# A macaron transformer layer in split fp32: step order of the down products, two loads, a layer norm and the block preparations are moved

## The chip, the cores and the metric

The kernel runs on one core of one Trainium2 chip. The metric is the device time of one execution in microseconds (us). TensorE (PE) multiplies, PEld is its weight load, VectorE is DVE, ScalarE is ACT, GpSimd is POOL, and SP issues nearly all DMAs. PSUM banks hold the sums that PE accumulates.

## The reference

One layer on x of 256 tokens by 2048 channels, in float32, every matrix product of full width:

```python
x = x + 0.5 * swiglu(rmsnorm(x, g1), w_gate, w_up, w_down)      # hidden width 5632
h = rmsnorm(x, gm)
q, k, v, u, vs, g_att, g_sg = split(h @ w_in)                   # 11776 columns
att = merge of 3 dilated causal window attentions (4 heads each) @ w_att_out
vs  = layernorm(gelu(vs)); sg = (gelu(u) * (tril(sg_w) @ vs + sg_b)) @ w_sg_out
x = x + (sigmoid(g_att) * att + sigmoid(g_sg) * sg) @ w_out
x = x + 0.5 * swiglu(rmsnorm(x, g2), w_gate2, w_up2, w_down2)
out = rmsnorm(x, gf)
```

Some 461 MB of weights are read from HBM once.

## The kernel before, in words

**Split products.** PE works on a rounded form of fp32. Each weight tile is therefore split in two: ACT copies it into `wh` (the rounded part, L351) and DVE writes `wl` = tile − `wh` (L66 is the line of a helper through which all DVE instructions go). The left side is kept as such a pair as well: `xhi`/`xlo` for normed x, `hA`/`hB` for the hidden layer, `mhi`/`mlo` for the merged branches. Each product is the sum of three matmuls of 128x512: high with `wh`, high with `wl`, low with `wh` (L358).

**Steps.** The products are cut into steps, and `lay_out` writes one list of all steps ahead of time. A plain step multiplies 256 rows of a 512-column weight strip with both halves of the tokens: 12 matmuls. Two neighbouring strips make a pair with four banks, `qd_0`, `qd_1` (first strip, token halves 0 and 1) and `qd_2`, `qd_3` (second strip). For a part of the rows a pair uses a seven-product scheme for 2x2 blocks in place of eight products: a *quad* with products p1 to p7, of 2 or 3 column groups each (6 or 9 matmuls). It loads four weight blocks (b11, b21, b12, b22, tiles `quads`, `part`, `vs`), and DVE forms sums of them: f, t2, t1 and t4 (tile `sum` holds t2 and then t4). It also needs sums of the left side's blocks (`forms`: `fx`, `fy`, `fh`, made by `sums_of` over a tile `fs`). p1, p6 and p7 stand near the end of the pair before (`opening`), p5, p4, p3 and p2 near the start of the pair itself (`closing`). After p1, p6, p7 and p5 a bank is read and moved or corrected by ACT or DVE before PE may add into it again: after p5, DVE writes `qd_2` = `qd_3` + something.

**Order within a pair.** The last argument of `gemm` that matters here is a pair (size, stage). With a stage function, plain steps are sorted by it: `PAIR` sorts the steps q of m in three stages (all but the last four, the next two, the last two), so that the steps of the first strip and of the second alternate by stage. It serves where the left side is still being made: x in four parts c = 0 to 3, the hidden layer by strips.

**Queues.** PE, ACT, DVE and SP each run their instructions in the order of the program. `split(i)` runs up to 5 steps ahead of PE, as far as a ring of 9 tiles of `wh`/`wl` has room. Five buffers of `raw` weights are refilled as splits free them. `at(e, fn)` puts a piece of work after step time e. `extra(wait, slack, cost, fn)` lets DVE work wait for a moment when its estimated load is low. `prepare_ready` forms the next block sum when the blocks it needs were issued 3 step times ago and DVE's load is low; `prepare_for` forces it when the split is due.

**x turned around.** Normed x is needed with channels on partitions. `turn` transposes 32x32 squares on DVE (`bt`), writes them to DRAM (`bm`, L471), reads them back shifted (L477, four DMAs `xt<-bmx` or `ga<-bmm`), and `ev` scales and splits them (`xt<-xt,gcols`, `xhi`, `xlo`). `turn_x` does so for a quarter c of x when a stage ends (n = 1: into the mixer; n = 2: into the second SwiGLU), `post_merge` for `m`. `sums_of` for n = 1 takes its tile `fs` from tag `gate`, two buffers that `bt` and `xt` use as well.

**The mixer's own loads.** At fixed step times after the mixer starts come the first quad blocks of the mixer (`gates`, +5), the spatial weights (+7) and the layer norm's rows (+10). The layer norm of `vs` is six pairs of DVE instructions (`nrm`).

Of the kernel before, what the change touches and what calls it, by code (L numbers as in the profile page):

```python
# [22 lines left out]
KD = D // P  # L23
FF = 5632
NC = 512
# [19 lines left out]
RAWB = 5  # L45
# [26 lines left out]
def layer(ctx: ExitStack, tc: tile.TileContext, a, out):  # L72
# [75 lines left out]
    def lay_out():  # L148
# [28 lines left out]
        for kind, s in steps:  # L177
            width = 2 if kind == "n" else s[0]["nq"]
            t += 1 if kind == "n" else width / 4
            ends.append(t)  # L180
            slots.append([(pos + q) % RING for q in range(width)])
            pos += width
            if kind == "n":
                hus.append(s)
                s[0]["steps"] += 1
            else:
                s[0]["gemms"][s[1] in ("p3", "p5", "p6", "p7", "p1")]["steps"] += 1
# [15 lines left out]

    PAIR = (2, lambda p, q, m: 2 if q >= m - 2 else q >= m - 4)
    BOTH = (2, None)
# [109 lines left out]
    def prepare_ready():  # L315
        for quad in started:
            if not quad["todo"]:
                continue
            what = quad["todo"][0]
            blocks, forms = NEEDS[what]  # L320
            if (all(quad["loaded"].get(b, 1e9) + 3 <= now[0] for b in blocks) and quad["split"].issuperset(forms)
                    and DVE.load + 0.56 * quad["nq"] * (NC / 512) <= FULL):
                assert all(b in quad["loaded"] for b in blocks)
                prepare_next(quad)
# [5 lines left out]

    started = []

    def form_of(quad, form):
# [211 lines left out]
    def residual(e, n, c, banks, scale, norm):  # L545
# [16 lines left out]

        turn_x(e + (6 if c == 1 else 2), n, c, 7 if c == 3 else 6)

    def turn_x(i, n, c, lag, read=3):
        def evac(src):
# [4 lines left out]
            split_psum(hi, lo, src, 1 if n and c < 3 else 0)  # L571
            tag = "gate" if n == 1 else "tmp"
            if c == CS[n]:
# [13 lines left out]
    def ffn(wg, wu, wd, down_post, group):  # L587
# [10 lines left out]
        for after, (part, quads_of) in zip(GATES, enumerate(PARTS)):  # L598
            for f in range(*after):
# [46 lines left out]
                quad = dict(k0=4 * CS[n], nq=2 if late else 3, forms=xT, home=merge if late else home)  # L646
                gemm(wg, f * NC, 0, KD, lhs_x, post_gate, BOTH if f else PAIR, bank, quad)
                gemm(wu, f * NC, 0, KD, lhs_x, post_up, BOTH, bank, quad)
# [67 lines left out]
    def post_gelu(key, j):  # L716
        def post(e, banks):
# [24 lines left out]
            if key == "vs":  # L742
                at(e + 2, st)
                if j == 2:
                    for t in range(NT):
                        for jj in range(3):
                            def nrm(t=t, jj=jj):
                                s = slice(jj * NC, (jj + 1) * NC)
                                v = mix["vs"][:, t, s]
                                DVE.scalar_tensor_tensor(v, v, mix["mv"][:, t, 0:1], mix["lng"][:, s],  # L750
                                                         op0=OP.subtract, op1=OP.mult)
                                DVE.scalar_tensor_tensor(v, v, mix["lnrs"][:, t:t + 1], mix["lnb"][:, s],
                                                         op0=OP.mult, op1=OP.add)
                            at(e + 4 + 3 * t + jj, nrm)
                    spatial_operands(e + 11)
# [257 lines left out]
    def post_merge(c):  # L1013
        def post(e, banks):
# [15 lines left out]

            turn(e + 2, f"m{c}", 8, put_tokens(lambda: ga), lambda: flat(ga), ev)
        return post

    front = [(o_s + j * NC, post_gelu("vs", j)) for j in range(3)] + [(o_u + j * NC, post_gelu("u", j)) for j in range(3)]
    for j, (c0, post) in enumerate(front):
        if j < 2:
            gemm(w_in, c0, 0, KD, lhs_x, post, PAIR if j == 0 else (1, None))
            continue
# [98 lines left out]
    at(88, masks)  # L1137
    at(mixer + 7, spatial_weights)
    at(mixer + 10, layer_norm_rows)
    for h in range(2):  # L1140
        sgw_turn(mixer + 13 + 8 * h, h)
    at(ends[-1] - 36, load_fin)
    for after, home in ((16, homes[0]), (mixer + 5, gates), (start_of(ffn2_gate) + 1, homes[1])):
        at(after, lambda home=home: move_in(home))
# [55 lines left out]

    loaded, done = RAWB + MORE, 3

# [98 lines left out]
```

## Time and profile before

| what | value |
|---|---|
| median of 3 runs | 2014.53 us (2013.36 to 2017.0) |
| the profiled execution's own time | 2012.44 us |
| its span, first to last instruction | 2010.7 us |
| mean granted TensorE clock | 0.995 |
| busy: PE, PEld, DVE, ACT, POOL | 1981.1, 1732.3, 1594.0, 1188.5, 52.5 us |
| HBM read | 461 MB, 244 GB/s with writes over the span |

The profile names a wait by the engine and tile that ended it. The stages lie thus in the span: first SwiGLU to about 700 us, the mixer's front to 970, attention to 1050, branches and merge to 1255, `w_out` to 1350, second SwiGLU to the end.

### The profile page before, as it was taken

What the parts mean: (1) busy time and instruction counts of PE and PEld (TensorE: products, weight loads), DVE (VectorE), ACT (ScalarE), POOL (GpSimd) and SP (SyncE); (2) the same over time, 40 slices, a digit from 0 to 9 for tenths busy, and PEclk for the clock granted to TensorE, in tenths of its full rate; (3) what the DMA queues carried; (4) which work ended last, traced back from release to release, by engine and by line L of the source; (5) the groups of instructions that cost most, each with busy time, mean ns of one, the idle gap of its engine ahead of it and who ended that gap; (6) DMA issues with size and microseconds to landing.
All of it is one profiled execution on the core that took longest, in us unless ns stands there. A gap on an engine that the chain in (4) does not pass through costs nothing.

```text
span 2010.7 us, 25179 instructions
## 1 busy us (share of the span) xinstructions
PE 1981.1 (99%) x9188; PEld 1732.3 (86%) x9188; DVE 1594.0 (79%) x1655; ACT 1188.5 (59%) x1382; POOL 52.5 (3%) x48
## 2 busy tenths in 40 slices
PE   9999999999999999999999999999999999999998
PEld 8887888888888888888888888888887888888887
DVE  6797889888887688676666777788987788888886
ACT  7565556665566566455554555576665566565664
POOL 0000010000000000000000000000000000000000
PEclk9999999999999999999999999999999999999999
DMA  9788778787776975888877667678887877888783
GB/s 324 251 285 250 228 234 269 246 253 250 248 243 214 281 270 187 232 292 254 266 237 246 217 201 232 202 254 265 262 252 228 247 242 250 241 246 259 246 264 125
DMA packets 264644, 492.34 MB, mean 245 GB/s; under 512 B 17484, under 2 KB 46024, under 8 KB 264392
## 3 DMA queue, kind: packets, MB, share of 16 engines
q1 hardware_dynamic: 253624, 469.49, 71.5%
q0 software_dynamic: 10576, 20.71, 5.9%
q8 instruction: 72, 1.18, 0.2%
q10 hardware_dynamic: 320, 0.53, 0.1%
q14 instruction: 52, 0.43, 0.1%
HBM read 461.01 MB, written 29.66 MB: 244 GB/s over the span
## 4 chain that ended last, share of the span: by engine, by line
PE 91%; DVE 3%; DMA 2%; issue 2%; ACT 2%; SPq 0%; POOLq 0%; POOL 0%; ACTq 0%; DVEq 0%
PE qd L358 68%; PE mm L358 22%; DVE wl L66 2%; DMA xt<-bmx 1%; ACT wh L351 1%; ACT xt L569 0%; DMA raw<-in_w_in_dram 0%; DVE quads L66 0%; DVE sum L66 0%; DMA part<-in_ffn_w_up_dram 0%; PE sp L805 0%; PE warm L1169 0%; DVE vs L66 0%; SPq L477 0%; PE pv L980 0%
## 5 line engine op out<-in xcount | busy, mean ns | idle before, releaser
L66 DVE TENSOR_TENSOR wl<-raw,wh 128x1024 fp32r<-128x1024 f32 (+1 forms) x636 | 694.6, 1111 | 185.7 <-ACT wh L351 180.7
L351 ACT ACTIVATE wh<-raw 128x1024 fp32r<-128x1024 f32 (+1 forms) x636 | 608.5, 966 | 364.4 <-PE qd L358 203.9
L358 PE MATMUL qd<-wl,xhi 128*128 128x512 f32 x1201 | 455.7, 379 | 0.3 <-DVE wl L66 0.3
L358 PE MATMUL qd<-wh,xhi 128*128 128x512 f32 x1201 | 455.6, 379 | 0.0
L358 PE MATMUL qd<-wh,xlo 128*128 128x512 f32 x1201 | 455.6, 379 | 0.0
L66 DVE TENSOR_TENSOR wl<-quads,wh 128x1536 fp32r<-128x1536 f32 (+2 forms) x226 | 290.9, 1301 | 159.4 <-ACT wh L351 159.1
L351 ACT ACTIVATE wh<-quads 128x1536 fp32r<-128x1536 f32 (+2 forms) x226 | 250.9, 1117 | 281.2 <-PE qd L358 266.6
L358 PEld LDWEIGHTS qd<-wl,xhi 128*128 128x128 f32 x1201 | 227.4, 189 | 32.5 <-DVE wl L66 0.7
L358 PEld LDWEIGHTS qd<-wh,xhi 128*128 128x128 f32 x1201 | 227.4, 189 | 32.0 <-issue 0.2
L358 PEld LDWEIGHTS qd<-wh,xlo 128*128 128x128 f32 x1201 | 227.4, 189 | 31.8
L358 PE MATMUL mm<-wh,xhi 128*128 128x512 f32 x608 | 232.4, 382 | 2.3 <-ACT wh L351 2.3
L358 PE MATMUL mm<-wh,xlo 128*128 128x512 f32 x608 | 231.6, 381 | 0.0
L358 PE MATMUL mm<-wl,xhi 128*128 128x512 f32 x608 | 229.4, 380 | 1.0 <-DVE wl L66 1.0
L358 PE MATMUL qd<-wh,hA 128*128 128x512 f32 x564 | 215.5, 382 | 7.5 <-DVE qd L66 7.5
L358 PE MATMUL qd<-wl,hA 128*128 128x512 f32 x564 | 215.3, 382 | 1.6 <-DVE wl L66 1.6
L358 PE MATMUL qd<-wh,hB 128*128 128x512 f32 x564 | 215.2, 382 | 0.0
L351 ACT ACTIVATE wh<-sum 128x1024 fp32r<-128x1024 f32 (+2 forms) x85 | 101.4, 1196 | 94.6 <-PE qd L358 67.0
L66 DVE TENSOR_TENSOR wl<-sum,wh 128x1024 fp32r<-128x1024 f32 (+2 forms) x85 | 117.8, 1394 | 21.7 <-ACT wh L351 20.1
L358 PEld LDWEIGHTS mm<-wh,xhi 128*128 128x128 f32 x608 | 115.7, 190 | 18.8 <-ACT wh L351 2.7
L358 PEld LDWEIGHTS mm<-wl,xhi 128*128 128x128 f32 x608 | 115.5, 190 | 17.4 <-DVE wl L66 1.3
L358 PEld LDWEIGHTS mm<-wh,xlo 128*128 128x128 f32 x608 | 115.5, 190 | 16.4 <-DVE xlo L66 0.2
L358 PEld LDWEIGHTS qd<-wh,hA 128*128 128x128 f32 x564 | 107.6, 191 | 23.5 <-DVE qd L66 8.3
(417 smaller groups left out, 2215.5 us busy)
## 6 DMA issues: line engine op xcount, KB each, us to landing
raw<-in_w_in_dram SPq DMA_DIRECT2D x168, 512.0 KB, 4.7
raw<-in_ffn_w_down_dram SPq DMA_DIRECT2D x120, 512.0 KB, 4.9
raw<-in_ffn_w_up_dram SPq DMA_DIRECT2D x112, 512.0 KB, 6.0
raw<-in_ffn_w_gate_dram SPq DMA_DIRECT2D x111, 512.0 KB, 4.2
quads<-in_ffn_w_gate_dram SPq DMA_DIRECT2D x38, 768.0 KB, 6.2
quads<-in_ffn_w_up_dram SPq DMA_DIRECT2D x38, 768.0 KB, 5.1
quads<-in_ffn_w_down_dram SPq DMA_DIRECT2D x32, 512.0 KB, 5.3
quads<-in_ffn_w_up_dram POOLq DMA_DIRECT2D x17, 768.0 KB, 10.8
```

The lines of the kernel that those rows point to most:

```text
L66: return method(out, *args, **kwargs)
L351: ACT.activation(wh, r[:, first:end], AF.Copy)
L358: PE.matmul(g["ps"][t], act, in_turn(w), start=not g["begun"][t], stop=g["left"][t] == 0, skip_group_check=g["quad"] is not None)
```

## The change

- `PAIR` now has two stages (all but the last two steps of each strip, then the last two). The old three stages are called `LATE` and stay for the two pairs that start from new x: `w_in` and the second SwiGLU's first strips.
- Quarter 3 of x for the mixer is scaled and split two step times later (9 in place of 7), and the `fs` tile for n = 1 comes from tag `tmp`.
- The mixer's first quad blocks are loaded one step time later, the spatial weights two, the layer norm's rows three.
- The layer norm's twelve DVE instructions become `extra` work with 3 steps of slack.
- A block sum that is due within two splits is *urgent*: it no longer waits three step times after its load was issued, nor for a low load.
- Quarter 3 of `m` is transposed one step time earlier, read back after 2 and split after 7 step times (3 and 8 before).

```diff
+            if kind == "s":
+                s[0].setdefault("at", {})[s[1]] = len(ends) - 1
...
-    PAIR = (2, lambda p, q, m: 2 if q >= m - 2 else q >= m - 4)
+    PAIR = (2, lambda p, q, m: q >= m - 2)
+    LATE = (2, lambda p, q, m: 2 if q >= m - 2 else q >= m - 4)
...
-            if (all(quad["loaded"].get(b, 1e9) + 3 <= now[0] for b in blocks) and quad["split"].issuperset(forms)
-                    and DVE.load + 0.56 * quad["nq"] * (NC / 512) <= FULL):
+            urgent = quad["at"]["p6" if what == "f" else next(f for f in USES if USES[f] == what)] - done <= 2
+            if (all(quad["loaded"].get(b, 1e9) + (0 if urgent else 3) <= now[0] for b in blocks)
+                    and quad["split"].issuperset(forms)
+                    and (urgent or DVE.load + 0.56 * quad["nq"] <= FULL)):
...
-        turn_x(e + (6 if c == 1 else 2), n, c, 7 if c == 3 else 6)
+        turn_x(e + (6 if c == 1 else 2), n, c, (9 if n == 1 else 7) if c == 3 else 6)
...
-            tag = "gate" if n == 1 else "tmp"
+            tag = "tmp"
...
-                gemm(wg, f * NC, 0, KD, lhs_x, post_gate, BOTH if f else PAIR, bank, quad)
+                gemm(wg, f * NC, 0, KD, lhs_x, post_gate, BOTH if f else LATE, bank, quad)
...
-                            at(e + 4 + 3 * t + jj, nrm)
+                            for fn in (centred, scaled):
+                                at(e + 4 + 3 * t + jj, lambda fn=fn: extra(0, 3, 0.7, fn))
...
-            turn(e + 2, f"m{c}", 8, put_tokens(lambda: ga), lambda: flat(ga), ev)
+            turn(e + (1 if c == 3 else 2), f"m{c}", 8, put_tokens(lambda: ga), lambda: flat(ga), ev,
+                 *((7, 2) if c == 3 else ()))
...
-    at(mixer + 7, spatial_weights)
-    at(mixer + 10, layer_norm_rows)
+    at(mixer + 9, spatial_weights)
+    at(mixer + 13, layer_norm_rows)
...
-    for after, home in ((16, homes[0]), (mixer + 5, gates), (start_of(ffn2_gate) + 1, homes[1])):
+    for after, home in ((16, homes[0]), (mixer + 6, gates), (start_of(ffn2_gate) + 1, homes[1])):
```

On PE the order of the matmuls differs at four places alone: the first and the last of the three down products of each SwiGLU. The first place, PE's rows where p5 of the first pair of down strips ends (`fh` is its left side), before and after:

```order
L358 MATMUL qd_3_1293<-wl,fh23.0_845 128x512
L358 MATMUL qd_3_1293<-wh,fh23.0_845 128x512
L358 MATMUL qd_2_1292<-wh,hA 128x512
L358 MATMUL qd_2_1292<-wl,hA 128x512
L358 MATMUL qd_2_1292<-wh,hB 128x512
```

```order
L363 MATMUL qd_3_1293<-wl,fh23.0_845 128x512
L363 MATMUL qd_3_1293<-wh,fh23.0_845 128x512
L363 MATMUL qd_0_1290<-wh,hA 128x512
L363 MATMUL qd_0_1290<-wl,hA 128x512
L363 MATMUL qd_0_1290<-wh,hB 128x512
```

The step after p5 was one of the second strip (`qd_2`); now a plain step of the first strip (`qd_0`, `qd_1`, 12 matmuls), p4 (9, into `qd_1`) and another plain step (12) come before it.

SP's DMAs where the mixer starts, before and after (`raw` are plain weight tiles, `quads` the four blocks of the mixer's first quad, `xt_3` the four pieces of the last quarter of turned x, `room` the spatial weights):

```order
L253 DMA raw_4969<-in_w_in_dram 128x2x512
L295 DMA quads<-in_w_in_dram 128x2x512 x4
L477 DMA xt_3_4996<-bmx_3_4927 32x4x256 x4
L253 DMA raw_5001<-in_w_in_dram 128x2x512
L253 DMA raw_5017<-in_w_in_dram 128x2x512
L695 DMA room<-in_sg_w_dram 128x12x128
```

```order
L256 DMA raw_4969<-in_w_in_dram 128x2x512
L482 DMA xt_3_4989<-bmx_3_4927 32x4x256 x4
L256 DMA raw_4994<-in_w_in_dram 128x2x512
L298 DMA quads<-in_w_in_dram 128x2x512 x4
L256 DMA raw_5017<-in_w_in_dram 128x2x512
L256 DMA raw_5033<-in_w_in_dram 128x2x512
```

The four pieces of x now stand ahead of the four blocks, with one plain tile between them; `room` comes two plain tiles later.

DVE's rows in `w_out`, where the last quarter of `m` (`ga458.75`) is split into `mhi` and `mlo`, as one piece of the difference (`quads<-quads,part` is f, `sum<-quads` t2, `quads<-sum,part` t1):

```order
 L66 TENSOR_TENSOR wl<-quads,wh 128x1024
-L66 TENSOR_TENSOR wl<-raw_9170,wh 128x1024
+L66 TENSOR_TENSOR quads<-quads,part 128x1024
+L66 TENSOR_TENSOR wl<-raw_9175,wh 128x1024
+L66 TENSOR_TENSOR sum<-quads 128x1024
+L66 TENSOR_TENSOR mlo<-ga458.75_8967,mhi 128x1024
 L66 TENSOR_TENSOR wl<-raw_9192,wh 128x1024
-L66 TENSOR_TENSOR quads<-quads,part 128x1024
-L66 TENSOR_TENSOR sum<-quads 128x1024
-L66 TENSOR_TENSOR wl<-sum,wh 128x1024
```

f and t2 move ahead of one `wl` each, and `mlo` from behind t1, two more `wl` and t4 to a place ahead of all of them. The transposes of this quarter move up by three rows earlier in the queue, and ACT's `mhi` by four rows.

More of the change, by code (lines that the diff above doesn't have):

```diff
@@ L320, in prepare_ready @@
             blocks, forms = NEEDS[what]
-            if (all(quad["loaded"].get(b, 1e9) + 3 <= now[0] for b in blocks) and quad["split"].issuperset(forms)
-                    and DVE.load + 0.56 * quad["nq"] * (NC / 512) <= FULL):
-                assert all(b in quad["loaded"] for b in blocks)
+            urgent = quad["at"]["p6" if what == "f" else next(f for f in USES if USES[f] == what)] - done <= 2
+            if (all(quad["loaded"].get(b, 1e9) + (0 if urgent else 3) <= now[0] for b in blocks)
+                    and quad["split"].issuperset(forms)
+                    and (urgent or DVE.load + 0.56 * quad["nq"] <= FULL)):
                 prepare_next(quad)
@@ L331, in layer @@
     started = []
+    done = 3
     def form_of(quad, form):
@@ L746, in post, with centred @@
                         for jj in range(3):
-                            def nrm(t=t, jj=jj):
+                            def centred(t=t, jj=jj):
                                 s = slice(jj * NC, (jj + 1) * NC)
@@ L751, in nrm, with scaled @@
                                                          op0=OP.subtract, op1=OP.mult)
+                            def scaled(t=t, jj=jj):
+                                s = slice(jj * NC, (jj + 1) * NC)
+                                v = mix["vs"][:, t, s]
                                 DVE.scalar_tensor_tensor(v, v, mix["lnrs"][:, t:t + 1], mix["lnb"][:, s],
                                                          op0=OP.mult, op1=OP.add)
-                            at(e + 4 + 3 * t + jj, nrm)
+                            for fn in (centred, scaled):
+                                at(e + 4 + 3 * t + jj, lambda fn=fn: extra(0, 3, 0.7, fn))
                     spatial_operands(e + 11)
@@ L1036, in layer @@
         if j < 2:
-            gemm(w_in, c0, 0, KD, lhs_x, post, PAIR if j == 0 else (1, None))
+            gemm(w_in, c0, 0, KD, lhs_x, post, LATE if j == 0 else (1, None))
             continue
@@ L1199, in layer @@
     at(12, lambda: norm_rstd(0))
-    loaded, done = RAWB + MORE, 3
+    loaded = RAWB + MORE
     def advance(i):
```

## The prediction

> **What bounds the kernel now.** I read the page's busy times first (PE 99% of the span, DVE 79%), then PE's table of waits, then the granted clock in short windows, and last the timeline around each wait of PE, with ACT, DVE and SP beside it. The waits of PE (what waited, for what: us in total, times, longest):
>
> ```profile
> PE qd L358 <- DVE qd L66: 7.5, 2, 3.8
> PE qd L358 <- DVE mlo L66: 2.7, 1, 2.7
> PE mm L358 <- ACT wh L351: 2.3, 1, 2.3
> PE qd L358 <- ACT qd L410: 2.2, 1, 2.2
> PE qd L358 <- DVE wl L66: 1.9, 2, 1.6
> PE qd L358 <- DVE vs L66: 1.7, 1, 1.7
> PE mm L358 <- DVE wl L66: 1.0, 1, 1.0
> ...
> PE qd L358 <- DVE part L66: 0.7, 1, 0.7
> PE qd L358 <- ACT mhi L456: 0.6, 1, 0.6
> ```
>
> PE bounds the kernel. It is idle inside its work for 7.5+2.7+2.3+2.2+1.9+1.7+1.0+0.7+0.6 = 20.6 us in all, in eleven places, and nothing but these waits can be won without taking matmuls away. But the busy time hides a second loss. The windows view (stretch, its length, busy us and instructions of PE, PEld, DVE, ACT, POOL, then the granted PE clock, DMA share, GB/s), taken behind six waits:
>
> ```profile
> 184.24:187.65 3.41, 3.41 (x9) 2.67 (x9) 0.00 (x0) 0.00 (x0) 0.00 (x0) 0.51 1.04 371
> ...
> 706.47:709.89 3.42, 3.42 (x9) 2.68 (x10) 3.42 (x4) 2.42 (x3) 0.00 (x0) 0.51 1.00 414
> 768.51:771.92 3.41, 3.41 (x16) 3.01 (x17) 3.34 (x5) 1.14 (x2) 0.00 (x0) 1.00 0.46 154
> 1286.74:1290.15 3.41, 3.22 (x8) 2.59 (x9) 1.27 (x2) 1.04 (x1) 0.00 (x0) 0.51 0.42 144
> 1334.53:1337.94 3.41, 3.41 (x10) 2.69 (x9) 3.37 (x5) 3.38 (x9) 0.00 (x0) 0.51 0.49 155
> 1515.43:1518.85 3.42, 3.18 (x8) 2.52 (x9) 0.19 (x1) 0.22 (x1) 0.00 (x0) 0.51 1.04 350
> ```
>
> After five waits the clock is halved for one stretch of 3.41 us: 9 matmuls go through in place of 16. Each costs 3.41 × (1 − 0.51) = 1.67 us, five cost 8.4. After the 1.7 us wait that ended at 768.51 the clock stayed full. So waits and their clock together are worth 20.6 + 8.4 = 29.0 us: that is the most the change can win. From the x16 row a matmul takes 3.41 / 16 = 0.213 us, a plain step of 12 takes 2.56.
>
> **The change part by part.** No matmul, split or byte is added or removed; instructions change places. So each term is a wait of PE, with its clock where it had one, less what is late next.
>
> *Down products (two of the four moved places hold a wait).* First the time from issue to landing (last number, median) of the DMAs that bring the last strip of the hidden layer back, then the timeline around the first wait:
>
> ```profile
> sg56.5_1284<-bmh63.75_1439 SPq DMA_DIRECT2D x4, 128.0 KB, 5.2
> ```
>
> ```profile
> 180.95 2.35 DVE L66 TENSOR_TENSOR wl<-raw,wh 128x1024 fp32r<-128x1024 f32 x2
> 183.22 0.69 DVE L66 TENSOR_TENSOR qd<-qd,quads 128x512 f32<-128x512 f32 x1
> 183.97 0.48 PE L358 MATMUL qd<-wh,hA 128*128 128x512 f32 x1 [3.73 <-DVE qd L66]
> 186.60 1.75 SPq L477 DMA_DIRECT2D sg56.5_1284<-bmh63.75_1439  x4
> ...
> 199.87 1.05 ACT L456 ACTIVATE hA<-sg56.5_1284 128x1024 fp32r<-128x1024 f32 x1
> ...
> 202.96 1.22 DVE L66 TENSOR_TENSOR hB<-sg56.5_1284,hA 128x1024 fp32r<-128x1024 f32 x1
> ```
>
> p5 ended at 183.97 − 3.73 = 180.24. DVE corrects `qd_2` only at 183.22 to 183.91, behind two splits, and the next step adds into that bank. After the change 12+9+12 = 33 matmuls stand between, 33 × 0.213 = 7.0 us: the bank is wanted at 187.3, 3.4 us after it is ready. Their weights are split by 183.3, as before, in the same places of the list. Late next could be the last strip of the hidden layer: its `hB` is done at 204.18. From 183.97 to the first step that reads it PE has 96 matmuls, 20.4 us, and 1.67 of slow clock: wanted at 206.1, 1.9 us to spare. PE comes 5.4 us earlier; `hA`, `hB` and the splits ahead of them wait for PE's ring and come along, but the DMA at 186.60 does not: it lands 5.2 us after its issue, so 191.8, and `hA` would start at 199.87 − 5.4 = 194.5. Covered. The second place (1515.67) has the same rows. Gain 7.5 + 2 × 1.67 = **10.8**; bounds 7.5 (the clock falls anyway) and 10.8. The last down products had no wait and keep their cover: 0. In `w_out` the new `PAIR` gives the old order, because the quad takes the two steps of the middle stage: 0.
>
> *`fs` tile and late x (entry to the mixer).*
>
> ```profile
> 657.04 0.43 DVE L66 TENSOR_TENSOR fsx<-xt 128x256 f32<-128x256 f32 x1 [3.55 <-DMA bmx<-btx]
> ...
> 687.67 2.06 SPq L295 DMA_DIRECT2D quads<-in_w_in_dram  x4
> 689.78 2.38 SPq L477 DMA_DIRECT2D xt<-bmx  x4
> ...
> 696.26 1.23 DVE L66 TENSOR_TENSOR quads<-quads 128x1024 f32<-128x1024 f32 x1 [1.69 <-DMA quads<-in_w_in_dram]
> 701.06 1.70 ACT L569 ACTIVATE xt<-xt,gcols 128x256 f32<-128x256 f32 x4 [7.75 <-DMA xt<-bmx]
> ...
> 704.85 0.48 PE L358 MATMUL mm<-wh,xhi 128*128 128x512 f32 x1 [2.28 <-ACT wh L351]
> ```
>
> DVE stood 3.55 us at 657 because the `fs` tile had to wait for a buffer that a DMA was still reading; the split behind it is PE's wait of 1.6 there (the longest of "DVE wl"). In tag `tmp` the tile has its own place: **1.6**, bounds 0 and 1.6. At the mixer ACT stood 7.75 us behind the read-back of x, with the next two `wh` behind it, and PE waited 2.3, then 1.0 for `wl`, then lost 1.67 of clock: 5.0. Now the read-back is issued at 687.67, ahead of the blocks, without the four blocks in front of it; two `wh` go ahead of it on ACT. The price: the blocks start at 687.67 + 2.38 + one issue of 0.4, so 690.5, the third at 691.5. The third block landed 696.26 − 688.7 = 7.6 us after its issue; again so, f starts at 699.1 on DVE and holds all `wl` behind it. f 1.22, then `wl` by 701.5: PE wants it at 704.85 − 2.28 = 702.57. But then t2, `wl`, t1 and `xlo` follow at 1.14 each, to 706.1, while the second step reads `xlo` at 702.57 + 2.56 + 0.43 = 705.6. A wait of 0.5 is left: **4.4**, bounds 5.0 and 1.8 (the blocks take 8.6 us, as `part` does below: 1.5 us of wait and a slow window).
>
> *Layer norm (768.51).* A windows row, then the timeline.
>
> ```profile
> 740.00:750.00 10.00, 10.00 (x48) 8.76 (x48) 7.08 (x6) 5.61 (x9) 0.00 (x0) 1.00 0.86 277
> ```
>
> ```profile
> 767.78 0.68 DVE L66 TENSOR_TENSOR vs<-vs,qd 128x512 f32<-128x512 f32 x1
> ...
> 768.51 0.48 PE L358 MATMUL qd<-wh,fx 128*128 128x512 f32 x1 [1.67 <-DVE vs L66]
> ```
>
> Here DVE is the short one (3.34 of 3.41 us busy in the row at 768.51 above). Three pairs of the layer norm stand ahead of the correction at 767.78 before and after; putting them off by a split each only lets the first `wl` pass (the other "DVE wl" wait, 0.3). What moves the correction is f of this quad, which comes two splits earlier, into the stretch where DVE had 2.9 of 10 us idle; all that follows moves up with it, and the correction needs 1.67. **1.9**, bounds 0 (its last block lands late, and DVE's idle time stays) and 2.0.
>
> *Last quarter of m (1283 to 1287).*
>
> ```profile
> 1266.58 2.78 SPq L477 DMA_DIRECT2D ga458.75_8967<-bmm  x4
> ...
> 1272.40 1.23 DVE L66 TENSOR_TENSOR wl<-quads,wh 128x1024 fp32r<-128x1024 f32 x1 [1.45 <-ACT wh L351]
> ...
> 1283.53 0.48 PE L358 MATMUL qd<-wh,mhi 128*128 128x512 f32 x1 [0.60 <-ACT mhi L456]
> ...
> 1285.66 1.22 DVE L66 TENSOR_TENSOR mlo<-ga458.75_8967,mhi 128x1024 fp32r<-128x1024 f32 x1
> ```
>
> ```profile
> part<-in_w_out_dram SPq DMA_DIRECT2D x1, 512.0 KB, 8.6
> ```
>
> PE wants `mhi` at 1283.53 − 0.60 = 1282.9, gets it 0.6 late and `mlo` 2.7 late: with the clock 5.0. The transposes move ahead of two `wl` and a correction, some 2.5 us, so the read-back at 1266.58 starts near 1264; its last piece, landing as slowly as the 8.6 of `part`, is there at 1275. The new order puts f straight behind a split that ends at 1273.6, but f reads `part`, which stands behind the read-back on SP now: issued at 1264 + 2.8 = 1266.8, there at 1275.4. From then f, `wl`, t2 and `mlo` at some 1.2 each end by 1280.2, the next `wl` by 1281.4: both before 1282.9. **5.0**; bounds 5.0 and 1.9 (`part` takes 3 us more: 1.5 of wait and a slow window).
>
> *Entry to the second SwiGLU.* A windows row first, then the timeline.
>
> ```profile
> 1320.00:1330.00 10.00, 10.00 (x48) 8.78 (x47) 9.96 (x14) 2.00 (x2) 0.00 (x0) 1.00 0.86 264
> ```
>
> ```profile
> 1329.48 1.21 DVE L66 TENSOR_TENSOR sum<-quads 128x1024 f32<-128x1024 f32 x1
> ...
> 1331.89 1.23 DVE L66 TENSOR_TENSOR wl<-sum,wh 128x1024 fp32r<-128x1024 f32 x1 [1.20 <-ACT wh L351]
> ...
> 1348.25 0.68 DVE L66 TENSOR_TENSOR part<-part,qd 128x512 f32<-128x512 f32 x1
> ```
>
> PE waited 2.2 for ACT's copy behind the `wh` of t2, lost 1.67 of clock, and 0.7 more at 1349 for `part`. t2 moves ahead of three other pieces of DVE work (`fx`, a `wl`, x's sums) and f further, about 3.5 us, so the first wait goes. But DVE has the same work up to `part` and is full here (9.96 of 10 us): only its idle 1.20 can be won. PE comes to that place 2.2 + 1.67 earlier and finds `part` 1.2 earlier: a wait of 0.7 + 3.9 − 1.2 = 3.4 takes the place of the two. What is gained is 1.2 less half a slow window: **0.4**, bounds −1.7 and 4.6. By the clock rule of the Trainium skill ("TensorE: Matmul & The Clock Gate", Part 1) the clock falls after an idle window of about 3.4 us in a free-running grid. This trace differs: 2.2 us was enough at 1333. By the rule a wait under 3.4 us would cost no clock, and the term would be 1.2 and the sum 0.8 larger.
>
> Sum: 10.8 + 1.6 + 4.4 + 1.9 + 5.0 + 0.4 = 24.1 us. The profiled execution took 2012.44, so 1988.3; the median of the runs lies 2.1 above it: **1990.4 us**.
>
> **The rivals.** *DVE hands the waits on.* DVE is full around 768 and 1325, and f now holds `wl` behind it until a block lands. Then PE gets the down products, the `fs` tile and half of what the mixer and m were worth: 10.8 + 1.6 + 2.2 + 0 + 2.5 − 1.7 = 15.4, so 1999.1. For it speaks the second SwiGLU's entry as worked out above; against it, at the mixer and at m I count 1 us and more to spare. *Only the step order counts.* Everything with a DMA in it stays: 10.8, so 2003.7. Against it speak the DVE waits, which name what was late. *Slower: urgent block sums stop DVE.* Before, a sum was formed three steps after its load was issued; now DVE may stand in front of a block under way, with all splits behind it. It turns the sign if the five moved block sums together lose the 24.1 and 4 more, 5.6 us each. A clock window is 1.67 of it, and PE has about 2 in hand, so each would have to land 6 us later than I assume, where the rows have 7.6 and 8.6. 4 us more than 2014.5 would be 2018.5.
>
> **How the numbers follow.** Forecast 0.70, DVE hands on 0.18, step order only 0.07, stopped by urgent sums 0.02, something that cancels all 0.03. About 0.2% (4 us) is what a measurement of this kernel can tell from no change. Faster 0.95, same 0.03, slower 0.02. The range: below, all waits and all slow windows gone, 2014.5 − 29.0 = 1985.5; above, all low ends but that of the down products (`fs` 0, mixer 1.8, layer norm 0, m 1.9, entry −1.7) give 12.8, so 2001.7. That takes in the first rival. 1986 to 2001.7.
>
> **What would show it.** Right: no wait of PE on "DVE qd", on `mlo`, `mhi` or "DVE vs"; no clock of 0.5 near 180, 697, 1272 or 1495; ACT's 7.75 in front of `xt` gone; a wait of 2 to 4 us for `part` near 1330. Wrong: DVE idle in front of f on a DMA of `quads` or `part`, PE waits on `wl` right behind it; a wait on `hA` or `hB` in the down products; `room` or `ln` late in front of DVE.

## The result, and the profile after

| | before | after |
|---|---|---|
| median of the runs shown with the result | 2013.94 us (4 runs, 2012.86 to 2017.0) | 1985.99 us (4 runs, 1984.81 to 1986.76) |
| the profiled execution's own time | 2012.44 us | 1985.29 us |
| its span | 2010.7 us | 1983.5 us |
| mean granted TensorE clock | 0.995 | 0.999 |
| busy PE | 1981.1 us | 1971.1 us |

The ratio is 0.9858 (95% interval 0.9841 to 0.9875), 28 us faster. The forecast was 1990.4; the time lies 4.4 us below it, and a hair under the low end of the range, 1986.0.

PE's waits in the changed kernel (what waited, for what: us in total, times, longest):

```profile
PE qd L363 <- DVE part L66: 1.0, 1, 1.0
PE qd L363 <- DVE xlo L66: 1.0, 2, 0.8
PE warm L1180 <- PEq L1295: 0.8, 1, 0.8
PE mm L363 <- DVE xlo L66: 0.8, 1, 0.8
PE qd L363 <- DVE wl L66: 0.6, 1, 0.6
```

Inside the work 1.0 + 1.0 + 0.8 + 0.6 = 3.4 us in five waits are left of 20.6 in eleven (the row with `warm` is the start of the kernel). Next the windows view at the places of the old waits, with the same columns as in the prediction, the granted clock third from the end:

```profile
178.00:182.00 4.00, 4.00 (x20) 3.52 (x19) 4.00 (x6) 2.47 (x3) 0.00 (x0) 1.00 0.98 218
696.00:704.00 8.00, 7.16 (x34) 5.96 (x33) 7.97 (x9) 5.73 (x9) 0.00 (x0) 1.00 0.60 202
1270.00:1276.00 6.00, 6.00 (x30) 5.25 (x29) 6.00 (x7) 3.35 (x5) 0.00 (x0) 1.00 0.54 182
1320.00:1330.00 10.00, 8.79 (x40) 7.05 (x39) 10.00 (x14) 8.64 (x12) 0.00 (x0) 1.00 0.79 236
1490.00:1496.00 6.00, 6.00 (x29) 5.28 (x28) 5.94 (x6) 3.97 (x5) 0.00 (x0) 1.00 1.05 247
```

None of the five stretches at half clock is left: the third number from the end is 1.00 in every row, and between 5.5 and 1978 us the trace has no other granted clock than full. At 696 and 1320, where PE still waits a little, DVE is busy in 7.97 of 8 and in 10.00 of 10 us.

The two executions run the same number of matmuls, and outside the four places of the down products in the same order. So the start of the k-th matmul before less its start after, read along the trace, gives the gain place by place:

| place | predicted | gained |
|---|---|---|
| first down products (184) | 5.4 | 5.7 |
| `fs` tile (658) | 1.6 | 1.9 |
| entry to the mixer (703) | 4.4 | 4.4 |
| layer norm's place (768) | 1.9 | 2.5 |
| last quarter of `m` (1283) | 5.0 | 5.5 |
| entry to the second SwiGLU (1305 to 1349) | 0.4 | 1.5 |
| second down products (1515) | 5.4 | 5.7 |
| start of the kernel | 0 | 0.2 |
| sum (from unrounded figures) | 24.1 | 27.2 |

Behind the last place nothing differs: from PE's last start to the end of the span it is 8.5 us in both.

**What a wait costs.** Each gain above is a little larger than its wait. PE's timeline at the mixer's entry of the changed kernel shows why (start, duration drawn, engine, instruction; in brackets the idle time and what ended it):

```profile
697.26 0.38 PE L363 MATMUL mm<-wh,xhi 128*128 128x512 f32 x1
697.48 0.38 PE L363 MATMUL mm<-wl,xhi 128*128 128x512 f32 x1
698.70 0.48 PE L363 MATMUL mm<-wh,xlo 128*128 128x512 f32 x1 [0.84 <-DVE xlo L66]
699.02 0.38 PE L363 MATMUL mm<-wh,xhi 128*128 128x512 f32 x1
```

Matmuls start 0.215 us apart, but one is drawn 0.38 long. The one that waited would have started at 697.48 + 0.215 = 697.70 and starts at 698.70, 1.00 later, where the bracket says 0.84; and the next comes 0.32 behind it, not 0.215. So a wait costs what its bracket says and 0.16 + 0.10 = 0.26 us more. The traces of before and after have 0.26 to 0.27 more at every wait in the work where the matmul that waited and the next one run at full clock. In a window at half clock matmuls start 0.427 us apart, so 8.0 go through where 15.8 would, and 7.8 × 0.216 = 1.69 us are lost. With these two prices the places close: first down products 3.73 + 0.26 + 1.69 = 5.68; `fs` 1.62 + 0.26 = 1.88; `m` 0.60 + 2.70 + 2 × 0.26 + 1.69 = 5.51.

### The profile page after: what moved, and what is told of

Read it like the earlier page. It is cut to its first block, busy times and chain, and to the rows that moved or that the text cites. A ratio compares the mean times of both kernels' runs of the same rounds, so it can differ in the third digit from the quotient of the medians.

```text
span 1983.5 us, 25183 instructions
## 1 busy us (share of the span) xinstructions
PE 1971.1 (99%) x9188; PEld 1723.6 (87%) x9188; DVE 1592.2 (80%) x1655; ACT 1189.5 (60%) x1382; POOL 51.7 (3%) x48
## 4 chain that ended last, share of the span: by engine, by line
PE 95%; DVE 2%; DMA 1%; issue 1%; ACT 0%; SPq 0%; POOLq 0%; POOL 0%; DVEq 0%; ACTq 0%
PE qd L363 71%; PE mm L363 22%; DVE wl L66 1%; DMA raw<-in_w_in_dram 0%; DMA quads<-in_w_in_dram 0%; DVE btx L66 0%; ACT wh L356 0%; PE sp L815 0%; PE warm L1180 0%; DMA xt<-bmx 0%; DVE xlo L66 0%; PE pv L990 0%; PE sc L953 0%; DVE x L66 0%; DVE quads L66 0%
## 5 line engine op out<-in xcount | busy, mean ns | idle before, releaser
L363 PE MATMUL qd<-wh,fx 128*128 128x512 f32 x352 | 119.2, 379 | 1.0 <-DVE part L66 1.0
```

Of the source, the lines that this page charges most:

```text
L363: PE.matmul(g["ps"][t], act, in_turn(w), start=not g["begun"][t], stop=g["left"][t] == 0, skip_group_check=g["quad"] is not None)
```

## The experiments

The times below are one run each where no interval stands; places are compared by the start of the same matmul, as above.

### The step order alone undone

```diff
-    PAIR = (2, lambda p, q, m: q >= m - 2)
+    PAIR = (2, lambda p, q, m: 2 if q >= m - 2 else q >= m - 4)
```

> The changed kernel with the old three stages in every pair of strips (only the step order is undone). Theory (the order gives 2 waits of 3.7 to 3.8 us and 2 half-clock windows away, and nothing else depends on it): the two waits on DVE's qd are back with a clock of 0.5 behind each, at the first and the second down products 5.7 us each, so 1985.3 + 11.3 = 1996.6 us. Rival (the clock would have stayed up anyway, only the waits count): 1985.3 + 7.5 = 1992.8. Rival (the time is caught up later, since DVE is the short one in the mixer): under 1990.

1996.54 us (4 runs, 1994.72 to 1998.62; ratio to before 0.9921, 0.9894 to 0.9947). From PE's waits and the windows view of this kernel:

```profile
PE qd L363 <- DVE qd L66: 7.5, 2, 3.8
```

```profile
184.09:187.50 3.41, 3.41 (x9) 2.69 (x9) 0.00 (x0) 0.00 (x0) 0.00 (x0) 0.50 1.04 374
1498.22:1501.64 3.42, 3.42 (x10) 2.66 (x9) 0.46 (x1) 0.63 (x1) 0.00 (x0) 0.50 1.04 367
```

Both waits and both half-clock stretches are back, and the two places lose 5.7 us each against the changed kernel's trace. The term stands, with its clock; the rival that counts the waits alone (1992.8) falls.

### The layer norm alone undone

```diff
-                            for fn in (centred, scaled):
-                                at(e + 4 + 3 * t + jj, lambda fn=fn: extra(0, 3, 0.7, fn))
+                            for fn in (centred, scaled):
+                                at(e + 4 + 3 * t + jj, fn)
```

> The changed kernel with the layer norm's twelve instructions at fixed step times again. Theory (the place at 768 us was won by the earlier f of the quad, as the prediction says): 0 to 0.3 us slower, 1985.3 to 1985.6, no wait on DVE's vs. Rival (the layer norm that stands back is what won the 2.4 us there): a wait of 1.7 us on DVE's vs near 760, 1987.7.

1983.28 us, 2 us under what was expected. PE has no wait on `vs`, and the layer norm's place costs nothing. The 2 us come from elsewhere: this execution had no wait at the mixer's entry and 0.2 in place of 0.8 at 1305, both behind a read-back (below). The layer norm that stands back earns nothing.

### The urgent sums alone undone

```diff
-            urgent = quad["at"]["p6" if what == "f" else next(f for f in USES if USES[f] == what)] - done <= 2
+            urgent = False
```

> The changed kernel where a block sum is never urgent: it waits three step times after its load and for a low load of DVE, as before. Theory (the urgent sums carry the layer norm's place, the second SwiGLU's entry and part of the last quarter of m): 2.4 us come back near 760, 1.5 to 2.2 near 1310 to 1330, and of the 5.4 at m between 0 and all, so 1989 to 1995. Rival (the sums only change places within DVE's spare time; the shifted loads and the layer norm carry the gain): 1985.3 to 1986.

1990.16 us. Its waits, then windows at two of them:

```profile
PE qd L363 <- ACT qd L415: 2.5, 1, 2.5
PE qd L363 <- DVE vs L66: 2.3, 1, 2.3
PE qd L363 <- DVE part L66: 1.0, 1, 1.0
...
PE qd L363 <- ACT part L417: 0.8, 1, 0.8
```

```profile
752.84:756.25 3.41, 1.15 (x6) 0.80 (x5) 3.41 (x4) 0.70 (x2) 0.00 (x0) 1.00 0.09 17
756.25:759.66 3.41, 3.41 (x10) 2.66 (x9) 3.38 (x5) 0.63 (x1) 0.00 (x0) 0.50 0.40 137
1312.63:1316.04 3.41, 1.58 (x8) 1.04 (x6) 2.21 (x3) 1.85 (x2) 0.00 (x0) 1.00 0.82 221
1316.04:1319.45 3.41, 2.72 (x13) 2.40 (x14) 3.41 (x5) 3.38 (x8) 0.00 (x0) 1.00 0.00 0
```

The layer norm's place loses 4.2 us: 2.27 + 0.26 + 1.69. The entry to the second SwiGLU loses 1.8 net: the wait for `qd` behind ACT that the kernel before had is back (2.52), and 0.75 behind ACT's `part`, in place of the changed kernel's 0.80, 0.55 and 0.17 for `xlo` and `wl`. So the urgent f and t2 carry both places, as the prediction said of f at 768. At `m` nothing is lost. Two waits of nearly one length, 2.27 and 2.52, do different things to the clock: the first halves it, the second does not. The waits of chosen lengths, below, take that up.

### The last quarter of m: its times, and both parts

```diff
-            turn(e + (1 if c == 3 else 2), f"m{c}", 8, put_tokens(lambda: ga), lambda: flat(ga), ev,
-                 *((7, 2) if c == 3 else ()))
+            turn(e + 2, f"m{c}", 8, put_tokens(lambda: ga), lambda: flat(ga), ev)
```

> The changed kernel with the last quarter of m transposed, read back and split at the old times. Theory (the 5.4 us near 1283 come from the earlier turn): waits on mhi and mlo are back with a half clock behind, 1985.3 + 5.4 = 1990.7. If f and t2, which now stand ahead, put mlo off further, up to 2.4 us more: 1993.1. Rival (the urgent f and t2 made the room, the turn's times do not matter): 1985.3 to 1986.

1985.79 us: one wait of 1.05 for `mlo`, 1.3 us lost at that place, and the clock stays. The theory of 1990.7 was wrong; the rival was right but for the 1.3 us. Three timelines show why: ACT's row for the copy of t2 in the kernel before, ACT's rows of this kernel, and DVE's of the changed kernel at the same place:

```profile
1280.02 1.06 ACT L351 ACTIVATE wh<-sum 128x1024 fp32r<-128x1024 f32 x1 [3.77 <-DVE sum L66]
```

```profile
1263.24 1.06 ACT L356 ACTIVATE wh<-sum 128x1024 fp32r<-128x1024 f32 x1 [1.58 <-PE qd L363]
1265.18 1.06 ACT L356 ACTIVATE wh<-raw 128x1024 fp32r<-128x1024 f32 x1 [0.89 <-PE qd L363]
1266.14 0.58 ACT L415 ACTIVATE qd<-qd 128x512 f32<-128x512 f32 x1
1266.66 1.04 ACT L461 ACTIVATE mhi<-ga458.75_8967 128x1024 fp32r<-128x1024 f32 x1
```

```profile
1261.41 1.23 DVE L66 TENSOR_TENSOR quads<-quads,part 128x1024 f32<-128x1024 f32 x1 [2.33 <-DMA part<-in_w_out_dram]
1262.55 1.22 DVE L66 TENSOR_TENSOR wl<-raw,wh 128x1024 fp32r<-128x1024 f32 x1
1263.68 1.22 DVE L66 TENSOR_TENSOR sum<-quads 128x1024 f32<-128x1024 f32 x1
1264.82 1.22 DVE L66 TENSOR_TENSOR mlo<-ga458.75_8967,mhi 128x1024 fp32r<-128x1024 f32 x1
```

With the old times `mhi` stands behind the copy of t2 (`wh<-sum`), as it did before. Before, that copy waited 3.77 us for DVE's t2; here it waits 1.58 for PE's ring, so t2 is no longer what holds ACT, and `mhi` is in time. With the new times (third fence) DVE does stand in front of f on `part`, 2.33 us, and `mlo` is in time all the same. If either part is enough, the place must be lost when both go:

```diff
+            urgent = False
+            turn(e + 2, f"m{c}", 8, put_tokens(lambda: ga), lambda: flat(ga), ev)
```

> The changed kernel with the last quarter of m at its old times and with no urgent sums: both parts that touch m are undone together (each alone cost 0 and 1.3 us there). Theory (either part is enough for the gain at m, so it is lost only when both are gone): waits on mhi (0.6) and mlo (2.7) near 1270 with a half clock behind, 5.4 us more than with urgent sums alone undone (1990.2): 1995.6. Rival (the parts add up): 1990.2 + 1.3 = 1991.5.

1996.04 us:

```profile
PE qd L363 <- DVE mlo L66: 2.7, 1, 2.7
...
PE qd L363 <- ACT mhi L461: 0.6, 1, 0.6
```

The two waits are those of the kernel before to a tenth, with a half clock behind them, and the place loses 5.3 us. The parts do not add up: one of them is enough.

### The fs tile's tag alone undone

```diff
-            tag = "tmp"
+            tag = "gate" if n == 1 else "tmp"
```

> The changed kernel with the fs tile for the mixer back in the tag of two buffers that the turned x uses. Theory: DVE stands 3.5 us in front of fsx again, PE waits 1.6 for wl near 650: 1.8 us more, 1985.3 + 1.8 = 1987.1, clock full. Rival (x's late read-back holds the buffers longer, the wait grows past 2 us and drops the clock): 1.8 + 1.7 and more, 1989 or above. Rival (the tag did nothing, PE's earlier arrival or an earlier read did it): 1985.3.

1987.89 us. PE's waits for `wl`, then DVE's first row on the tile:

```profile
PE qd L363 <- DVE wl L66: 2.2, 2, 1.6
```

```profile
651.44 0.42 DVE L66 TENSOR_TENSOR fsx<-xt 128x256 f32<-128x256 f32 x1 [3.55 <-DMA bmx<-btx]
```

DVE's stall is back, 3.55 us as before, and PE's wait with it: the place loses 1.9 us = 1.62 + 0.26, and a wait of 0.56 for `wl` at 681, not seen in the kernel before, loses 0.8 more. The clock stays full. The term stands.

### The mixer's entry: one part, the other, both

Quarter 3 of x split at 7 step times, the loads as in the change:

```diff
-        turn_x(e + (6 if c == 1 else 2), n, c, (9 if n == 1 else 7) if c == 3 else 6)
+        turn_x(e + (6 if c == 1 else 2), n, c, 7 if c == 3 else 6)
```

> The changed kernel with quarter 3 of x scaled and split at the old 7 step times; the mixer's loads stay shifted. Theory (the shifted loads, which let the read-back go first, win the mixer's entry): the read-back lands 9 us after its issue near 680, ACT finds it there, and at most 0.5 us is lost, 1985.3 to 1985.8, or 0.8 us less since xlo stands earlier on DVE. Rival (the late split is what wins, since x holds two wh behind it on ACT): wh 2.3 and wl 1.0 late and a half clock, up to 1985.3 + 4.4 = 1989.7.

1986.03 us, no wait at the entry (1.1 us gained there against the changed kernel's trace, and lost again to 0.4 on `vs` near 753 and to 1.8 in place of 0.8 for `xlo` at 1306). The loads at the old step times, x split late:

```diff
-    at(mixer + 9, spatial_weights)
-    at(mixer + 13, layer_norm_rows)
+    at(mixer + 7, spatial_weights)
+    at(mixer + 10, layer_norm_rows)
...
-    for after, home in ((16, homes[0]), (mixer + 6, gates), (start_of(ffn2_gate) + 1, homes[1])):
+    for after, home in ((16, homes[0]), (mixer + 5, gates), (start_of(ffn2_gate) + 1, homes[1])):
```

> The changed kernel with the mixer's first blocks, spatial weights and layer norm rows loaded at the old step times (the blocks stand ahead of the read-back of x again); quarter 3 of x stays at 9 step times. Theory (the loads win): the read-back lands some 10 us later, x is ready 1.3 us after PE wants it and xlo a little later still; 1.5 to 2.5 us without a half clock, 4.4 with one: 1987 to 1989.7. Rival (the late split alone is enough, as two wh pass ahead of x): 1985.3 to 1985.8.

1983.1 us, no wait at the entry either, though the blocks stand ahead of the read-back again. My theory had 1.5 to 2.5 us lost here; the rival was right in what it forecast. Then both undone, by the two diffs above:

> The changed kernel with both parts at the mixer's entry undone: the mixer's loads at the old step times and quarter 3 of x split after 7 step times (each alone cost nothing there). Theory (either is enough): the waits for wh (2.3) and wl (1.0) are back, with a half clock behind them: 5.3 us more than a run without any wait at that entry (1983.1 us), so 1988.4. Rival (the urgent sums have made the room on DVE, the two parts do nothing): 1983 to 1986, no half clock near 700.

1985.86 us, no half clock, as the rival had it: the entry loses 2.1 us, not 5.3. The rival's reason was that another part of the change had made the room. Two kernels built up from the one before test that: the step order and the tag alone, and the urgent sums alone.

> The kernel before with two of the changed kernel's parts alone: the step order and the fs tile's tag. All DVE and DMA parts at the mixer, the layer norm, m and the second SwiGLU's entry are as before. Theory A (the mixer's entry is won by the loads, the late split or the urgent sums): its waits of 2.3 and 1.0 and its half clock stay, 2012.4 - 11.4 - 1.9 = 1999.1. Theory B (without the stall at fsx, DVE, ACT and SP come to the mixer's entry up to half a microsecond earlier for PE, and the read-back lands a microsecond sooner or later by itself, which decides whether the wait passes 2.0 us in one window): the wait for wh is under 1 us there and the clock stays, 1995.5 to 1997. In both: waits on vs near 760, on mhi and mlo near 1275, on ACT's qd near 1323.

> The kernel before with the urgent sums alone. Theory (they carry the layer norm's place 2.3, four of the 5.4 at m and 1.5 to 2.2 at the second SwiGLU's entry, and nothing at the mixer's entry): 2012.4 - 8 = 2004.4, with the waits on DVE's qd (3.7 and 3.8), on wl near 659 (1.6) and on wh near 705 (2.3) as before. Rival (they also make the room at the mixer's entry): 2001, no half clock near 706.

2001.36 and 2010.27 us. ACT's row on quarter 3 of x and the wait of PE behind it, in the run with both parts undone, in the one with order and tag, and in the one with urgent sums:

```profile
691.21 1.71 ACT L574 ACTIVATE xt<-xt,gcols 128x256 f32<-128x256 f32 x4 [5.64 <-DMA xt<-bmx]
695.00 0.48 PE L363 MATMUL mm<-wh,xhi 128*128 128x512 f32 x1 [0.17 <-ACT wh L356]
```

```profile
695.21 1.70 ACT L574 ACTIVATE xt<-xt,gcols 128x256 f32<-128x256 f32 x4 [7.07 <-DMA xt<-bmx]
699.00 0.79 PE L363 MATMUL mm<-wh,xhi 128*128 128x512 f32 x1 [4.14 <-ACT wh L356]
```

```profile
706.29 1.70 ACT L574 ACTIVATE xt<-xt,gcols 128x256 f32<-128x256 f32 x4 [6.67 <-DMA xt<-bmx]
710.09 0.79 PE L363 MATMUL mm<-wh,xhi 128*128 128x512 f32 x1 [4.21 <-ACT wh L356]
```

In all three ACT stands in front of the read-back with two `wh` behind it, as before the change (7.75). What differs is when the read-back lands, and PE's wait with it: 0.17, 4.14, 4.21, and 2.28 in the trace of before. The rival's reason falls: the wait is there, and longer, in the two kernels that have the other parts. The traces say it more sharply. The run with both parts undone and the one with order and tag have the same instructions in the same order on PE, ACT, DVE, SP and POOL up to 730 us, since the urgent sums move nothing before that; so do before and the run with urgent sums alone up to 742. Within each pair nothing but the execution differs at the entry. My first reading, that both parts undone must lose 5.3, falls as well. What the entry loses without either part hangs on when the read-backs land: PE's wait for `wh` goes from 0.2 us to 4.2 with two windows at half clock.

Is either part enough, or were these executions lucky? The slowest read-back of the four without either part was used 9.2 us after its last issue (worked out at the end). With the loads alone moved, the last piece is issued at 680.26. An estimate with 9.2 us lets ACT start at 689.5; PE's first matmul follows 3.8 us later, as in the rows above, at 693.3, and PE wants it at 694.8. In the three executions with the late split and the old loads (this one and two below) ACT comes to x 9.6 to 10.8 us after the last issue, and it never stood in front of it. So either part covers every landing seen here, though the first rests on one execution and this estimate. With either part in place, six of the thirteen executions here still waited 0.6 to 1.4 us for `xlo` at the entry, and seven not at all.

The same two runs give the other terms alone. With order and tag, 5.7 us are gained at each of the down products and 1.9 at `fs`; the waits on `vs` (1.67), `mhi` and `mlo` (0.6, 2.7) are unchanged. With urgent sums, 2.5 are gained at the layer norm's place, 4.1 at `m` and 2.4 at the second SwiGLU's entry, 9.0 in all where 8 was expected. But the trace is only 2.2 us shorter than that of before, since other places lost more in this execution: `fs` waited 3.4 (1.6 before) and the mixer's entry 4.2 (2.3), and the half clock behind the down products lasted two windows both times, 1.4 and 1.2 us more.

### Waits of chosen lengths, and the clock

In one plain step of four in the two SwiGLUs, two small matmuls of zeros are added with `k` GpSimd memsets of their tile between them (`k` goes through twelve values from 8 to 32):

```diff
+    def hold_pe(i):
...
+        PE.matmul(b, hold, hold[:, 0:32], start=False, stop=False, skip_group_check=True)
+        for _ in range(k):
+            POOL.memset(hold, 0.0)
+        PE.matmul(b, hold, hold[:, 0:32], start=False, stop=False, skip_group_check=True)
```

> The changed kernel with some 50 waits added in plain steps of the two SwiGLUs: a small matmul of zeros, then 8 to 32 GpSimd memsets of the tile that it read, then a second one that reads the tile again, so that TensorE stands idle for some 1 to 5 us. They add zero to a bank. The question is which waits halve the clock. Theory (a grid of 3.413 us runs free, and a window halves the clock of the next when TensorE was idle for more than about 2.0 to 2.1 us inside that one window): waits under 2.0 us never drop it, waits over 4.2 us always do, and between these it goes by how the wait falls on the grid; each drop costs 1.7 us. Rival (the length of the wait alone decides, from 2.2 us on): no wait over 2.3 us keeps the clock. Rival (a whole window must be idle): no wait under 3.4 us drops it, all over 6.8 us do.

2309.86 us with 45 added waits of 2.2 to 8.5 us. The windows view, cut along the grid of this execution (the clock changes only at times that differ by whole multiples of 3.413):

```profile
71.20:74.61 3.41, 1.18 (x8) 0.98 (x8) 3.05 (x2) 0.33 (x1) 1.64 (x8) 1.00 0.15 58
74.61:78.02 3.41, 3.41 (x10) 2.69 (x9) 3.06 (x5) 1.06 (x1) 0.00 (x0) 0.50 0.02 5
101.92:105.33 3.41, 1.73 (x9) 1.23 (x7) 2.25 (x3) 1.06 (x1) 1.23 (x6) 1.00 0.32 70
105.33:108.75 3.42, 1.83 (x9) 1.64 (x10) 0.00 (x0) 0.00 (x0) 1.23 (x6) 1.00 0.83 316
108.75:112.16 3.41, 3.41 (x17) 2.98 (x16) 1.46 (x1) 2.97 (x4) 1.65 (x2) 1.00 0.24 15
...
91.68:95.09 3.41, 2.86 (x8) 2.32 (x9) 0.00 (x0) 0.00 (x0) 0.41 (x2) 0.50 0.01 3
95.09:98.51 3.42, 3.42 (x18) 2.99 (x17) 1.23 (x1) 2.25 (x4) 0.00 (x0) 1.00 0.00 0
255.52:258.93 3.41, 2.76 (x8) 2.22 (x9) 1.07 (x1) 0.00 (x0) 0.48 (x3) 0.50 0.45 154
258.93:262.35 3.42, 3.42 (x10) 2.69 (x9) 0.82 (x1) 1.06 (x1) 0.00 (x0) 0.50 0.00 0
```

The first wait, 71.36 to 73.56, lies in one window: 2.20 us, and the next window runs at half clock. The second, 103.67 to 106.92, is longer, 3.25 us, but falls 1.66 into one window and 1.59 into the next: the clock stays. So both rivals fall, the one by length alone and the one that wants a whole idle window.

Counting PE's idle time of 0.1 us and more window by window (from 0.215 us behind the start of the last matmul, 0.43 at half clock) in the eight traces that have half-clock windows inside the work: of 149 windows at full clock with idle time 60 were followed by one at half clock, those with 2.000 us idle or more; the other 89 had 1.997 or less. Of 63 windows at half clock 34 were followed by another one, those with 0.776 or more idle, and 29 by full clock, with 0.685 or less. The last four rows show this second bound: 0.69 idle in the first, full clock behind it; 0.79 in the second, half clock behind it (the view itself has 0.14 us less idle time in each, since a matmul is drawn longer than the distance between starts). No window among the 212 goes against the two bounds, and in the other nine traces, which stay at full clock, no window has more than 1.96 idle. (Other ways of counting idle time would shift the bounds a little.) It also settles the pair above: in the run without urgent sums the wait of 2.27 lies wholly in 752.84 to 756.25, which has 2.5 us idle, and the wait of 2.52 leaves 1.997 idle in 1312.63 to 1316.04 and 0.79 in the next. And it says why the down products' wait of 3.7 us cost one half-clock window in the trace of before and two in the run with urgent sums: there 3.28 us lay in one window and 0.78 in the next.

By the Trainium skill ("TensorE: Matmul & The Clock Gate", Part 1) the window is 3413 ns and free-running, and the runs agree with both. It has the clock fall after at least one idle window; these runs differ: 2.0 us of idle time within a window are enough.

### Three small waits, and two parts left out

```diff
-        turn_x(e + (6 if c == 1 else 2), n, c, (9 if n == 1 else 7) if c == 3 else 6)
+        turn_x(e + (6 if c == 1 else 2), n, c, (9 if n == 1 else 7) if c == 3 else 7 if n == 2 and c == 0 else 6)
```

together with the layer norm at fixed times and the mixer's loads at the old ones.

> The changed kernel with three small things: the layer norm at fixed times and the mixer's loads at the old times (in the runs with one of these alone no wait stood at the mixer's entry), and the first quarter of x for the second SwiGLU scaled one step time later, so that ACT does not stand in front of its read-back with the next copy behind it. Theory: the waits for xlo near 698 (0.8) and 1305 (0.2 to 1.8, with the read-back's landing) are gone, those for wl (0.5) and part (1.0) stay: 1.5 to 3 us under the changed kernel of the same job, 1982 to 1984.5. Rival (these waits come and go between executions whatever the order): no difference that can be told, within 1 us.

> The changed kernel itself, to know its scatter beside the others: 1985 to 1987 us, with a wait for xlo at the mixer's entry that is there or not (0 to 1 us), and one near 1305 of 0 to 1.8 us.

1988.35 us (4 runs, 1987.68 to 1988.7; ratio 0.9875, 0.9861 to 0.989) against 1985.2 (4 runs, 1983.89 to 1986.08; 0.9858, 0.9842 to 0.9874) of the changed kernel in the same job: worse, not better. ACT no longer waits for the read-back, but the late split of x came out on DVE behind the sums of x, f, t2 and t1:

```profile
1305.83 1.22 DVE L66 TENSOR_TENSOR quads<-sum,part 128x1024 f32<-128x1024 f32 x1
1306.97 1.22 DVE L66 TENSOR_TENSOR xlo<-xt,xhi 128x1024 fp32r<-128x1024 f32 x1
...
1308.24 0.79 PE L363 MATMUL qd<-wh,xlo 128*128 128x512 f32 x1 [4.18 <-DVE xlo L66]
```

Without that line, with the layer norm and the loads as before alone:

> The changed kernel without two of its parts: the layer norm at fixed times and the mixer's loads at the old times; the late split of x, its tag, the urgent sums, the step order and m's earlier turn stay. Theory (both parts earn nothing; the three runs with the loads or the layer norm as before had no wait at the mixer's entry): 1983 to 1984.5, up to 2 us under the changed kernel's 1985.2 to 1986.0. Rival (the small waits there come and go): 1985 to 1986.

1985.23 us (4 runs, 1984.72 to 1985.57; ratio to before 0.985, 0.9833 to 0.9866): no different from the changed kernel. So I take the single times of 1983.1 and 1983.28 above for executions in which the read-backs landed early, not for better orders. The two parts earn nothing that can be measured, and nothing tried here beats the changed kernel.

## Why the prediction came out as it did

**Right: where the time was and which edit takes it.** Every wait named was gone, with all five half-clock stretches; nothing came in front of `hA`, `hB` or the forms. The order of the steps gives 5.7 at each place (undone alone, and done with the tag alone). The `fs` tile gives 1.9. At the layer norm's place it is the earlier f, not the layer norm.

**Right in size, wrong in what it hung on: mixer and `m`.** "Now the read-back is issued at 687.67, ahead of the blocks" is true (it is at 679.51 in the changed kernel, the blocks at 682.14), and so is "two `wh` go ahead of it on ACT", but each alone keeps the clock up; likewise at `m` the earlier turn and the urgent sums. I had put them into one sum as if each were needed. DVE's order behind the blocks was read rightly: f starts at 691.74, and `xlo` comes out behind t2 and t1, late as forecast. That the term of 4.4 was met to the tenth is luck, though. The old entry cost 5.5 in this trace and not 5.0, and the wait left for `xlo` took 1.1 and not 0.5, so two misses cancel. And the 2.3 us that the term started from is one execution's: in four executions with the old order at the entry PE's wait for `wh` was 0.2 to 4.2.

**The step that failed: a wait was priced at its bracket.** It is in the sentence "waits and their clock together are worth 20.6 + 8.4 = 29.0 us: that is the most the change can win", and in every term of the sum. The brackets of the eleven waits leave out 0.26 us each, 2.9 in all: the most that can be won is 20.6 + 2.9 + 5 × 1.69 = 31.9 us. The changed kernel's trace bears this out: 27.2 gained, and the five waits left cost 3.4 + 5 × 0.26 = 4.7 us, 31.9 together. So the low end should have been 2014.5 − 31.9 = 1982.6. The median of 1985.99 lies above even the 1985.5 that was worked out, but that was rounded up to 1986 as the low end, so the range is missed by 0.01 us; what was off is the sum.

**The terms that were too small.** 27.2 was gained in the trace, 24.1 summed. The second SwiGLU's entry is the largest part, 1.1 us: I had 3.4 us of wait for `part` and half a slow window left; there were 0.80, 0.55, 0.17 and 1.04 for `xlo` (twice), `wl` and `part`. DVE is full there as predicted, but what it owes is spread over four places, and none of the four comes near 2.0 us in one window. Of the other 2.0, the 0.26 us of each wait make up 1.8: order 0.5, `fs` 0.3, layer norm 0.6, `m` 0.4. The last 0.2 are at the start of the kernel, where nothing was changed.

**The step from the profiled execution to the median.** I added 2.1 us, the distance before. After it is 0.7. The runs of the kernel before spread from 2009.07 to 2017.85 over all jobs, those of the changed kernel from 1983.89 to 1986.76, and the two waits that vary most between executions, at the mixer's entry and at `fs`, are among those that the change takes away; so is the half clock behind the down products, which lasts one window or two. That they make the spread fits their sizes (0.2 to 4.2, 1.6 to 3.4, and 1.2 to 1.4 for each second window), but the single runs have no trace to show it. So 3.1 of the 4.4 us are the sum's, and 1.4 this step's.

**The rivals.** DVE does not hand the waits on: the urgent f did stop DVE, for 2.33 us at `m`, but cost nothing there. That only the order counts is refuted by 1996.54 with the order undone, 17 us under before.

## What to carry to other kernels

Price a wait of the bounding engine by the starts of its instructions, not by the bracket, and ask where it falls on the clock's grid: it is cheap as long as less than 2.0 us of it lie in one window of 3.41 us, so that two short waits may cost less than one of the same sum. When two edits guard the same spot, undo them one at a time and together before either gets the credit. A wait that ends with a DMA's landing is a spread, not a number: look at more than one execution before it goes into a sum or is taken for an improvement.

## What the hardware showed that was not expected

- The clock bounds are sharp: 2.00 us idle in a full-clock window halves the next one, and a half-clock window goes back to full only with about 0.7 us idle or less (212 windows, no exception). So half clock is easier to stay in than to fall into, and a second short wait right behind the first one prolongs it: in the runs with order and tag and with urgent sums the rest of the wait for `wh` at the mixer's entry and 0.66 for `wl` behind it left 1.7 and 2.3 us idle in the first slow window, and a second slow window followed.
- A wait at full clock costs 0.26 us more than its bracket, the same at every place.
- The read-back of x at the mixer's entry takes its own time. SP's rows for its four pieces, with both parts undone and with order and tag alone:

```profile
681.48 2.00 SPq L482 DMA_DIRECT2D xt<-bmx  x4
```

```profile
683.34 2.67 SPq L482 DMA_DIRECT2D xt<-bmx  x4
```

  ACT used them at 691.21 and at 695.21, so 7.7 and 9.2 us after the last issue (683.48, 686.01). The last issue itself was 2.5 us later in the second, with the same instructions ahead of it; the two traces part at the read-back before this one, which ACT used at 661.24 and at 662.55. PE lost 2.1 us at the entry in the first and 8.0 in the second.
